# A SwiGLU's gate and up projections as a 2x2 block product with seven half products

## The chip, the cores and the metric

The kernel runs on one core of a Trainium2 chip. Its metric is the device time of one execution in microseconds. Five engines with queues of their own take part: TensorE (PE, matmuls, with its weight loads shown apart as PEld), VectorE (DVE), ScalarE (ACT), GpSimd (POOL) and SyncE (SP, which here only issues the transfers). The kernel has TensorE write into eight banks of PSUM, 128 x 512 float32 each; all other data is worked on in SBUF.

## The reference: what is computed

Two layers, each a feed-forward block (FFN1), a mixer and a second feed-forward block (FFN2), on 512 tokens of width 1024, all in float32. A feed-forward block is

```python
def swiglu_ffn(h, w_gate, w_up, w_down):
    return (jax.nn.silu(h @ w_gate) * (h @ w_up)) @ w_down
```

with h = rms_norm(x), w_gate and w_up of 1024 x 2816 and w_down of 2816 x 1024; its result is normalised again, halved and added to x. So each block has 22 column tiles of 128 (2816 = 22 x 128) in gate and in up. The mixer (attention, a convolution and gated linear attention, joined by gates) isn't touched by the change.

## The kernel before, in words

**Products in three parts.** The operands of most matmuls are of the type F32R, and float32 data is split in two for it: `split` (L109) casts it to F32R on ScalarE (`hi`, L110) and lets VectorE subtract that from the original (`lo`, L111). A product is hi x hi + hi x lo + lo x hi, three matmuls. The normalised input stands transposed in SBUF as `xh` and `xl` (L101, 102), 8 tiles of 128 of the width by 512 tokens.

**Weights.** `load_w` (L113) fetches 128 x 1024 float32 into `raw` (three buffers), and splits them into `whi` and `wlo` (five buffers each). `proj_cols` (L136) loads a column tile of 128, and `mm_cols` (L130) runs 8 x 3 matmuls of 128 x 128 stationary weights against 512 tokens, into one bank.

**A feed-forward block** is `ffn` (L267). Its first two column tiles go the other way round (L278 to 287): the tokens are stationary, 128 at a time, and 256 columns of weights move (`mm_tok`, L161, bank `pf`), since the input arrives token tile by token tile: `arrive[i]()` (L205) transposes token tile i on TensorE into banks `pt` and splits them into xh and xl, between the matmuls. The results `ht` are transposed later (L299). The other 20 column tiles are the loop of L289:

```python
pg = proj_cols(wg, f * P, "pg")
pu = proj_cols(wu, f * P, "pu")
nc.scalar.activation(h, pg, AF.Silu)
nc.vector.tensor_tensor(h, pu, h, op=ALU.mult)
```

The 22 results `hid` are then split by `stat` (L304) into `sh` and `sl` and multiplied with w_down in `out_proj` (L226), which keeps eight banks open, for four token tiles by two halves of the width. As each token tile ends there, `finish` (L831) applies the norm after the block, adds to x and starts the norm before the next block (`pre_norm`, L193).

**Buffers.** Tiles of 128 x 512 come from four groups of slots (L27): t 16, b 4, q 10, s 14. Banks come from two groups (L28): pa 2, pb 6. A slot or buffer is handed on when its last reader is done.

**Order.** Matmuls and transposes are held in the order of the text (L65 to 69). All other instructions are put in order at build time by the framework's planner, which goes by the order of the text among those whose inputs and buffers are free by its own estimate of times. Each engine then works its queue strictly in that order, and waits on semaphores where something is not ready. Transfers are all issued from SP's queue, in order as well.

Of the kernel before, what the change touches and what calls it, by code (L numbers as in the profile page):

```python
# [8 lines left out]
F32 = mybir.dt.float32  # L9
F32R = mybir.dt.float32r  # L10
AF = mybir.ActivationFunctionType
ALU = mybir.AluOpType

P = 128
D = 1024
S = 512
NT = S // P
KC = D // P
DFF = 2816
NF = DFF // P  # L20
# [21 lines left out]
def kernel(  # L42
# [9 lines left out]
    nc = tc.nc  # L52
# [5 lines left out]
    wp = ctx.enter_context(tc.tile_pool(name="wp", bufs=5))  # L58
    tp = ctx.enter_context(tc.tile_pool(name="tp", bufs=1))
# [5 lines left out]
    def mm(*a, **k):  # L65
        tc.keep_in_program_order(nc.tensor.matmul(*a, **k))  # L66

    def transpose(*a):
        tc.keep_in_program_order(nc.tensor.transpose(*a))

    def slot(name, dt=F32, tag="t"):
        return tp.tile([P, 512], dt, tag=tag, name=name, bufs=SLOTS[tag])

    def bank(n, tag="pb"):
        return psp.tile([P, 512], F32, tag=tag, name=n, bufs=BANKS[tag])


    ident = const.tile([P, P], F32, name="ident")
# [11 lines left out]
    for c in range(2):  # L90
        blk = strict[:, c * CHUNK:(c + 1) * CHUNK]
        r = slice(c * CHUNK, (c + 1) * CHUNK)
# [8 lines left out]
    xh = resid.tile([P, KC, S], F32R, name="xh")  # L101
    xl = resid.tile([P, KC, S], F32R, name="xl")
# [6 lines left out]
    def split(hi, lo, src):  # L109
        nc.scalar.copy(hi, src)  # L110
        nc.vector.tensor_tensor(lo, src, hi.bitcast(F32), op=ALU.subtract)  # L111

    def load_w(parts, n):  # L113
        raw = wp.tile([P, 1024], F32, tag="raw", name="raw", bufs=3)
        for view, src in parts:
            nc.sync.dma_start(view(raw), src)
        hi = wp.tile([P, 1024], F32R, tag="whi", name="whi")
        lo = wp.tile([P, 1024], F32R, tag="wlo", name="wlo")
        split(hi[:, :n], lo[:, :n], raw[:, :n])
        return hi, lo  # L120

    def load_cols(w2d, c0, width=P):
        kc = w2d.shape[0] // P
        n = kc * width
        hi, lo = load_w([(lambda r: r[:, :n].rearrange("p (k c) -> p k c", c=width),
                          w2d[:, c0:c0 + width].rearrange("(k p) c -> p k c", p=P))], n)
        v = lambda t: t[:, :n].rearrange("p (k c) -> p k c", c=width)
        return v(hi), v(lo)

    def mm_cols(ps, wh, wl, ks=range(KC)):  # L130
        for k in ks:
            mm(ps, wh[:, k, :], xh[:, k, :], start=(k == 0), stop=False)
            mm(ps, wh[:, k, :], xl[:, k, :], start=False, stop=False)
            mm(ps, wl[:, k, :], xh[:, k, :], start=False, stop=(k == KC - 1))

    def proj_cols(w2d, c0, name, tag="pb"):  # L136
        wh, wl = load_cols(w2d, c0)
        ps = bank(name, tag)
        mm_cols(ps, wh, wl)
        return ps  # L140
# [30 lines left out]
    def load_g(row):  # L171
        g = gp.tile([P, D], F32, tag="g", name="g")
        nc.sync.dma_start(g, row.unsqueeze(0).broadcast_to([P, D]))
        return g
# [5 lines left out]
    def rms(srcs):  # L180

        ss = sm.tile([P, 2], F32, tag="ss", name="ss")
        for h in range(2):
            nc.scalar.activation(junk, srcs[h], AF.Square, scale=1.0 / 32.0, accum_out=ss[:, h:h + 1])
        ms = sm.tile([P, 1], F32, tag="ms", name="ms")
        nc.vector.tensor_scalar(ms, ss[:, 0:1], ss[:, 1:2], EPS, op0=ALU.add, op1=ALU.add)
        rs = sm.tile([P, 1], F32, tag="rs", name="rs")
        nc.gpsimd.tensor_tensor(rs, ms, mhalf[:, 0:1], op=ALU.pow)
        return rs

    HS = [slice(h * HALF, (h + 1) * HALF) for h in range(2)]

    def pre_norm(i, gB, pooled=()):  # L193
        t = slice(i * P, (i + 1) * P)
        hns = [slot("hn", tag="b") for j in range(2)]
        for j in pooled:
            nc.gpsimd.tensor_tensor(hns[j], x_sb[i][:, HS[j]], gB[:, HS[j]], op=ALU.mult)
        rs = rms([x_sb[i][:, c] for c in HS])
        for j in range(2):
            if j in pooled:  # L200
                nc.scalar.mul(hns[j], hns[j], rs)
            else:
                nc.vector.scalar_tensor_tensor(hns[j], x_sb[i][:, HS[j]], rs, gB[:, HS[j]], op0=ALU.mult, op1=ALU.mult)

        def arrive():  # L205
            for j, hn in enumerate(hns):
                pt = bank("pt")
                for k in range(4):
                    transpose(pt[:, k * P:(k + 1) * P], hn[:, k * P:(k + 1) * P], ident)
                src = pt.rearrange("p (k t) -> p k t", t=P)  # L210
                split(xh[:, 4 * j:4 * j + 4, t], xl[:, 4 * j:4 * j + 4, t], src)

        return arrive

# [43 lines left out]
        return w  # L258


    def ffn_weights(wg, wu):
        return load_kcols(wg, 0, 256), load_kcols(wu, 0, 256)

    def mixer_weights(W):
        return load_kcols(W, C_V, 512)

    def ffn(wg, wu, wd, weights, arrive, finish, upcoming, early, begin):  # L267

        if begin is None:
            wgt, wut = weights  # L270
        else:
            wgt = load_kcols(wg, 0, 256)
            begin(0)
            wut = load_kcols(wu, 0, 256)
            begin(1)
            arrive[0]()
        hk = []
        for i in range(NT):  # L278
            pf = bank("pf", "pb")
            mm_tok(pf[:, 0:256], i, wgt)  # L280
            if i + 1 < NT:
                arrive[i + 1]()
            mm_tok(pf[:, 256:512], i, wut, first=False)
            h = slot("ht", tag="s")
            nc.scalar.activation(h[:, 0:256], pf[:, 0:256], AF.Silu)
            nc.vector.tensor_tensor(h[:, 0:256], pf[:, 256:512], h[:, 0:256], op=ALU.mult)
            hk.append(h)
        hid = [None, None]
        for f in range(2, NF):  # L289
            pg = proj_cols(wg, f * P, "pg")  # L290
            pu = proj_cols(wu, f * P, "pu")
            h = slot("hid", tag="t" if f < 18 else "q")
            nc.scalar.activation(h, pg, AF.Silu)
            nc.vector.tensor_tensor(h, pu, h, op=ALU.mult)  # L294
            hid.append(h)
            if f < 4:
                pt = bank("pth", "pa")
                for i in range(NT):
                    transpose(pt[:, i * P:(i + 1) * P], hk[i][:, (f - 2) * P:(f - 1) * P], ident)  # L299
                h = slot("hid", tag="q")  # L300
                nc.scalar.copy(h, pt)
                hid[f - 2] = h

        def stat(f):  # L304
            sh, sl = slot("sh", F32R, "s"), slot("sl", F32R, "s")
            split(sh, sl, hid[f])
            return sh, sl

        return out_proj(wd, NF, stat, TAIL, finish, upcoming, early)
# [500 lines left out]

    load_x(0)
    g0 = load_g(norm_pre[0, 0])
    arrive = [pre_norm(0, g0)]

    def begin(n):
        if n == 0:
            load_x(1)
            arrive.append(pre_norm(1, g0))
        else:
            load_x(2)  # L820
            load_x(3)
            arrive.extend(pre_norm(i, g0) for i in (2, 3))

    weights = None
    subs = [(l, s) for l in range(L) for s in range(3)]
    for idx, (l, s) in enumerate(subs):
        gpost = load_g(norm_post[l, s])
        gnext = load_g(norm_pre[subs[idx + 1][0], subs[idx + 1][1]]) if idx + 1 < len(subs) else None
        upcoming = []

        def finish(i, banks):  # L831
            post_norm(i, banks, gpost, 1.0 if s == 1 else 0.5)
            if gnext is not None:
                upcoming.append(pre_norm(i, gnext, (1,) if i < 2 else ()))
            else:
                for h in range(2):
                    nc.sync.dma_start(out[0, i * P:(i + 1) * P, HS[h]], x_sb[i][:, HS[h]])

        early = None
        if idx + 1 < len(subs):  # L840
            l1, s1 = subs[idx + 1]
            early = ((lambda: ffn_weights(f1g[l1], f1u[l1])), (lambda: mixer_weights(w_in[l1])),
                     (lambda: ffn_weights(f2g[l1], f2u[l1])))[s1]
        if s == 0:
            weights = ffn(f1g[l], f1u[l], f1d[l], weights, arrive, finish, upcoming, early,
                          begin if idx == 0 else None)
        elif s == 1:
            weights = mixer(l, weights, arrive, finish, upcoming, early)
        else:
            weights = ffn(f2g[l], f2u[l], f2d[l], weights, arrive, finish, upcoming, early, None)  # L850
        arrive = upcoming


# [27 lines left out]
```

## Time and profile before

| | |
|---|---|
| median of three timed runs | 2432.33 us (2432.09 to 2432.5) |
| the profiled execution, its own time | 2432.07 us |
| its span in the profile | 2430.0 us |
| TensorE busy / weight loads busy | 2410.4 us / 2013.2 us |
| VectorE busy | 1186.6 us |
| ScalarE busy | 846.1 us |
| mean granted TensorE clock | 0.998 |
| read from memory | 227.32 MB |

An engine's busy time counts its own instructions; the lengths of matmuls are modelled and overlap, so what one matmul costs is read from a stretch of many, length by count. The chain of waits goes back from the last instruction to what released each step, and shows so which engine set the end. "Idle before" in a row is the time that the engine stood still ahead of these instructions, with what ended it.

### The profile page before, as it was taken

How to read it: one execution, taken by the hardware profiler on the slowest of the kernel's cores; microseconds unless marked ns; L12 is line 12 of the kernel's file. 1: busy time of each engine (PE TensorE's matmuls, PEld its weight loads, DVE VectorE, ACT ScalarE, POOL GpSimd, SP SyncE). 2: the span in 40 equal slices, each digit the busy share in tenths (PEclk: the TensorE clock that was granted, in tenths of full speed). 3: DMA queues.
4: the chain of work that ended last, by engine and by line, in shares of the span. 5: the costliest groups of instructions: out<-in, count | busy, mean ns of one | idle time of the engine just before them, and what ended most of it. 6: DMA issues, size and time to landing. Idle time of an engine off the chain costs nothing.

```text
span 2430.0 us, 28558 instructions
## 1 busy us (share of the span) xinstructions
PE 2410.4 (99%) x11528; PEld 2013.2 (83%) x11528; DVE 1186.6 (49%) x1551; ACT 846.1 (35%) x1340; POOL 174.7 (7%) x282
## 2 busy tenths in 40 slices
PE   8999999999999999999999999999999999999998
PEld 7888888887888898888888888888878888888887
DVE  4322336858965353223353223378599644432233
ACT  4222226644323342222342222366433334322222
POOL 0000001201011100000000000012010211000000
PEclk9999999999999999999999999999999999999999
DMA  6333333231333243333243333241313332333331
GB/s 185 97 101 96 96 96 107 64 87 52 106 87 104 78 122 96 96 98 98 82 122 96 96 97 97 85 119 53 96 53 104 96 104 80 112 95 96 100 98 62
DMA packets 304692, 231.27 MB, mean 95 GB/s; under 512 B 9290, under 2 KB 281708, under 8 KB 304560
## 3 DMA queue, kind: packets, MB, share of 16 engines
q1 hardware_dynamic: 304560, 229.45, 32.1%
q8 instruction: 90, 1.47, 0.3%
q14 instruction: 42, 0.34, 0.0%
HBM read 227.32 MB, written 2.10 MB: 94 GB/s over the span
## 4 chain that ended last, share of the span: by engine, by line
PE 99%; ACT 0%; DMA 0%; DVE 0%; SPq 0%; issue 0%; DVEq 0%; POOLq 0%; ACTq 0%
PE o L66 23%; PE pu L66 18%; PE pg L66 18%; PE gate L66 11%; PE pb L66 5%; PE pf L66 4%; PE pa L66 2%; PE gr L66 2%; PE pv L66 2%; PE q L66 2%; PE gv L66 2%; PE k L66 2%; PE pgl L66 2%; PE gk L66 1%; PE gq L66 1%; PE z L66 1%
## 5 line engine op out<-in xcount | busy, mean ns | idle before, releaser
L110 ACT CAST whi<-raw 128x1024 fp32r<-128x1024 f32 x418 | 438.0, 1049 | 1033.5 <-PE pg L66 325.6
L111 DVE TENSOR_TENSOR wlo<-raw,whi 128x1024 fp32r<-128x1024 f32 x418 | 519.8, 1246 | 564.1 <-ACT whi L110 553.2
L66 PE MATMUL o<-whi,sh 128*128 128x512 f32 x704 | 274.1, 389 | 0.0
L66 PE MATMUL o<-whi,sl 128*128 128x512 f32 x704 | 273.9, 389 | 0.0
L66 PE MATMUL o<-wlo,sh 128*128 128x512 f32 x704 | 273.9, 389 | 0.0
L66 PE MATMUL pg<-xh,whi 128*128 128x512 f32 x640 | 249.8, 390 | 0.0
L66 PE MATMUL pg<-xh,wlo 128*128 128x512 f32 x640 | 249.1, 389 | 0.0
L66 PE MATMUL pg<-xl,whi 128*128 128x512 f32 x640 | 249.0, 389 | 0.0
L66 PE MATMUL pu<-xh,wlo 128*128 128x512 f32 x640 | 249.0, 389 | 0.0
L66 PE MATMUL pu<-xh,whi 128*128 128x512 f32 x640 | 249.0, 389 | 0.0
L66 PE MATMUL pu<-xl,whi 128*128 128x512 f32 x640 | 249.0, 389 | 0.0
L294 DVE TENSOR_TENSOR hid<-pu,hid 128x512 f32<-128x512 f32 x80 | 55.3, 692 | 273.5 <-PE pu L66 273.5
L481 DVE SCALAR_TENSOR_TENSOR y<-u,cw,y 128x511 f32<-128x511 f32 (+14 forms) x240 | 164.3, 747 | 0.0
L111 DVE TENSOR_TENSOR sl<-hid,sh 128x512 fp32r<-128x512 f32 x88 | 60.1, 690 | 198.0 <-ACT sh L110 198.0
L66 PEld LDWEIGHTS o<-whi,sl 128*128 128x128 f32 x704 | 132.1, 188 | 27.5
L66 PEld LDWEIGHTS o<-wlo,sh 128*128 128x128 f32 x704 | 132.1, 188 | 27.4
L66 PEld LDWEIGHTS o<-whi,sh 128*128 128x128 f32 x704 | 132.1, 188 | 27.3
L66 PE MATMUL gate<-xh,whi 128*128 128x512 f32 x384 | 151.3, 394 | 0.0
L66 PE MATMUL gate<-xl,whi 128*128 128x512 f32 x384 | 149.6, 390 | 0.0
L66 PE MATMUL gate<-xh,wlo 128*128 128x512 f32 x384 | 149.5, 389 | 0.0
L66 PEld LDWEIGHTS pu<-xh,wlo 128*128 128x128 f32 x640 | 120.1, 188 | 25.1
L66 PEld LDWEIGHTS pg<-xh,wlo 128*128 128x128 f32 x640 | 120.1, 188 | 25.0
(219 smaller groups left out, 3927.2 us busy)
## 6 DMA issues: line engine op xcount, KB each, us to landing
raw<-in_w_in_dram SPq DMA_DIRECT2D x108, 512.0 KB, 3.9
raw<-in_ffn_w_gate_dram SPq DMA_DIRECT2D x88, 512.0 KB, 3.9
raw<-in_ffn_w_up_dram SPq DMA_DIRECT2D x88, 512.0 KB, 3.9
raw<-in_ffn_w_down_dram SPq DMA_DIRECT2D x88, 512.0 KB, 3.5
raw<-in_w_branch_dram SPq DMA_DIRECT2D x24, 512.0 KB, 3.3
raw<-in_w_out_dram SPq DMA_DIRECT2D x16, 512.0 KB, 3.3
g<-in_norm_pre_dram SPq DMA_DIRECT2D x6, 512.0 KB
g<-in_norm_post_dram SPq DMA_DIRECT2D x6, 512.0 KB, 5.3
```

Of the source, the lines that this page charges most:

```text
L66: tc.keep_in_program_order(nc.tensor.matmul(*a, **k))
L110: nc.scalar.copy(hi, src)
L111: nc.vector.tensor_tensor(lo, src, hi.bitcast(F32), op=ALU.subtract)
L294: nc.vector.tensor_tensor(h, pu, h, op=ALU.mult)
L481: nc.vector.scalar_tensor_tensor(y[:, back:], u[:, :S - back], cw[:, c, j:j + 1], y[:, back:], op0=ALU.mult, op1=ALU.add)
```

## The change

Column tiles 3 to 21 (19 of 22) of gate and up are computed together, as one block product per tile. Let A11 and A12 be the upper and lower 512 rows of the gate's 128 columns, A21 and A22 those of up's, and B11, B21 the two halves of the width for tokens 0 to 255, B12, B22 for tokens 256 to 511. Wanted are gate = (A11 B11 + A12 B21, A11 B12 + A12 B22) and up likewise with A21 and A22: eight half products. The change forms

- S1 = A21 + A22, S2 = S1 + A11, S3 = A11 + A21, S4 = S2 + A12, from the weights, for each unit (a unit is one column tile);
- T1 = B11 - B12, T2 = -T1 - B22, T3 = T2 + B11, T4 = T2 + B21, from the input, once per block;
- seven products: A11 B11, S3 T3, S2 T2, A12 B21, S1 T1, A22 T4, S4 B22, each of 4 x 3 matmuls of 256 tokens.

Three banks A, B and C serve a unit. S2 T2, S1 T1 and S4 B22 are added in A to what A11 B11 has left there, and ScalarE copies A out after the first three of these four (p1, u2, u4), and C after S3 T3 (p7); A22 T4 is added in C. Three VectorE sums put the four results together, silu is applied to the two halves of gate, and one product ends the unit.

`Forms` holds the T: for the first two token tiles the transposes are kept in float32 (`xr`, ScalarE), for the last two VectorE makes the T tile by tile (16 sums of 128 x 256), and `finish` splits them (eight of 128 x 512), placed behind the transposes of the first two column tiles. T1 to T3 stand in 12 slots of the group s and T4 in the four of b until the last unit; the float32 forms and `xr` take 12 of the group t for a while.

`Ring` splits the seven sums and weights of a unit, two to a buffer of whi and wlo, so that a unit takes three and a half of these; the pairing of an even unit differs from that of an odd one. Raw weights come in two buffers of 3072 (one per unit, four transfers of 256 KB; elsewhere they are used in thirds) in place of three of 1024. The `unit`'s copies lie in two new tiles `cp`. Column tile 2 stays as it was, and the transposes of the first two tiles stand between its gate and its up. The buffer for descriptors that the framework sets aside in SBUF is made smaller.

```diff
--- before.py
+++ after.py
@@ -110,10 +110,20 @@
         nc.scalar.copy(hi, src)
         nc.vector.tensor_tensor(lo, src, hi.bitcast(F32), op=ALU.subtract)
 
-    def load_w(parts, n):
-        raw = wp.tile([P, 1024], F32, tag="raw", name="raw", bufs=3)
+    thirds = []
+
+    def load_raw(parts):
+        if not thirds:
+            r = wp.tile([P, 3, 1024], F32, tag="raw", name="raw", bufs=2)
+            thirds.extend(r[:, j] for j in range(3))
+        raw = thirds.pop(0)
         for view, src in parts:
             nc.sync.dma_start(view(raw), src)
+        return raw
+
+    def load_w(parts, n):
+        raw = load_raw(parts)
         hi = wp.tile([P, 1024], F32R, tag="whi", name="whi")
         lo = wp.tile([P, 1024], F32R, tag="wlo", name="wlo")
         split(hi[:, :n], lo[:, :n], raw[:, :n])
...
         def arrive():
+            pts = []
             for j, hn in enumerate(hns):
                 pt = bank("pt")
                 for k in range(4):
                     transpose(pt[:, k * P:(k + 1) * P], hn[:, k * P:(k + 1) * P], ident)
                 src = pt.rearrange("p (k t) -> p k t", t=P)
                 split(xh[:, 4 * j:4 * j + 4, t], xl[:, 4 * j:4 * j + 4, t], src)
+                pts.append(src)
+            if forms is not None:
+                forms.arrive(i, pts)
 
         return arrive
...
+    class Forms:
+        def __init__(self):
+            self.first = []
+            self.raw = None
+            self.parts = {}
+
+        def arrive(self, i, pts):
+            if i < 2:
+                row = [slot("xr").rearrange("p (k t) -> p k t", t=P) for src in pts]
+                for r, src in zip(row, pts):
+                    nc.scalar.copy(r, src)
+                self.first.append(row)
+                return
+            if self.raw is None:
+                self.raw = {n: [slot(n).rearrange("p (k t) -> p k t", k=2) for c in range(2)]
+                            for n in ("T1", "T2", "T3", "T4")}
+            first = self.first[i - 2]
+            tok = slice((i - 2) * P, (i - 1) * P)
+            for c in range(2):
+                k = slice(2 * c, 2 * c + 2)
+                t1, t2 = (self.raw[n][c][:, :, tok] for n in ("T1", "T2"))
+                nc.vector.tensor_tensor(t1, first[0][:, k], pts[0][:, k], op=ALU.subtract)
+                nc.vector.scalar_tensor_tensor(t2, t1, -1.0, pts[1][:, k], op0=ALU.mult, op1=ALU.subtract)
+                for j, n in enumerate(("T3", "T4")):
+                    nc.vector.tensor_tensor(self.raw[n][c][:, :, tok], t2, first[j][:, k], op=ALU.add)
+
+        def finish(self):
+            for n, tag in (("T3", "s"), ("T2", "s"), ("T1", "s"), ("T4", "b")):
+                hi = [slot(n + "h", F32R, tag).rearrange("p (k t) -> p k t", k=2) for c in range(2)]
+                lo = [slot(n + "l", F32R, tag).rearrange("p (k t) -> p k t", k=2) for c in range(2)]
+                for c in range(2):
+                    split(hi[c], lo[c], self.raw[n][c])
+                self.parts[n] = [(hi[k // 2][:, k % 2], lo[k // 2][:, k % 2]) for k in range(4)]
+            for n, k0, t0 in (("B11", 0, 0), ("B21", 4, 0), ("B22", 4, 256)):
+                self.parts[n] = [(xh[:, k0 + k, t0:t0 + 256], xl[:, k0 + k, t0:t0 + 256]) for k in range(4)]
+
+    class Ring:
+        def __init__(self):
+            self.n = 0
+
+        def put(self, src):
+            two = len(src.shape) == 3
+            if self.n % 2 == 0:
+                self.hi, self.lo = (wp.tile([P, 1024], F32R, tag=t, name=t).rearrange("p (f c) -> p f c", f=2)
+                                    for t in ("whi", "wlo"))
+            h = self.n % 2
+            assert not (two and h)
+            self.n += 2 if two else 1
+            f = slice(0, 2) if two else slice(h, h + 1)
+            split(self.hi[:, f], self.lo[:, f], src if two else src.unsqueeze(1))
+            v = lambda t: t.rearrange("p (k c) -> p k c", c=P)
+            r = [(v(self.hi[:, j]), v(self.lo[:, j])) for j in range(f.start, f.stop)]
+            return r if two else r[0]
+
+    H0, H1 = slice(0, 256), slice(256, 512)
+
+    def unit(w0, w1, c0, forms, ring, h):
+        r = wp.tile([P, 6, 512], F32, tag="raw", name="raw", bufs=2)
+        for w, q0 in ((w0, 0), (w1, 2)):
+            for j in range(2):
+                nc.sync.dma_start(r[:, q0 + 3 * j].rearrange("p (k c) -> p k c", c=P),
+                                  w[j * 512:(j + 1) * 512, c0:c0 + P].rearrange("(k p) c -> p k c", p=P))
+        add = lambda o, a, b: nc.vector.tensor_tensor(o, a, b, op=ALU.add)
+        add(r[:, 1:5:3], r[:, 0:6:5], r[:, 2:3].broadcast_to([P, 2, 512]))
+        add(r[:, 2], r[:, 4], r[:, 0])
+        A, B, C = bank("A"), bank("B"), bank("C")
+
+        def product(w, n, ps, first):
+            wh, wl = w
+            for k, (fh, fl) in enumerate(forms.parts[n]):
+                for j, (a, b) in enumerate(((wh, fh), (wh, fl), (wl, fh))):
+                    mm(ps[:, H0], a[:, k], b, start=(first and k == 0 and j == 0), stop=False, skip_group_check=True)
+
+        cp = [tp.tile([P, 512], F32, tag="cp", name="cp", bufs=2) for _ in range(2)]
+        p1, p7, u2, u4 = cp[0][:, H0], cp[0][:, H1], cp[1][:, H0], cp[1][:, H1]
+        put = ring.put
+        even = ring.n % 2 == 0
+        if even:
+            a11, s3 = put(r[:, 0:2])
+            s2, a12 = put(r[:, 2:4])
+        else:
+            a11 = put(r[:, 0])
+            s3, s2 = put(r[:, 1:3])
+        product(a11, "B11", A, True)
+        nc.scalar.copy(p1, A[:, H0])
+        add(r[:, 0], r[:, 2], r[:, 3])
+        if even:
+            s1, a22 = put(r[:, 4:6])
+        else:
+            a12, s1 = put(r[:, 3:5])
+        product(s3, "T3", C, True)
+        nc.scalar.copy(p7, C[:, H0])
+        product(s2, "T2", A, False)
+        nc.scalar.copy(u2, A[:, H0])
+        if even:
+            s4 = put(r[:, 0])
+        else:
+            s4, a22 = put(r[:, 0:6:5])
+        product(a12, "B21", B, True)
+        add(h[:, H0], B[:, H0], p1)
+        nc.scalar.activation(h[:, H0], h[:, H0], AF.Silu)
+        product(s1, "T1", A, False)
+        nc.scalar.copy(u4, A[:, H0])
+        product(a22, "T4", C, False)
+        nc.vector.tensor_tensor(u2, C[:, H0], u2, op=ALU.subtract)
+        nc.vector.tensor_tensor(u4, p7, u4, op=ALU.subtract)
+        product(s4, "B22", A, False)
+        nc.scalar.activation(h[:, H1], A[:, H0], AF.Silu)
+        nc.vector.tensor_tensor(h, cp[1], h, op=ALU.mult)
...
-        hid = [None, None]
-        for f in range(2, NF):
-            pg = proj_cols(wg, f * P, "pg")
-            pu = proj_cols(wu, f * P, "pu")
-            h = slot("hid", tag="t" if f < 18 else "q")
-            nc.scalar.activation(h, pg, AF.Silu)
-            nc.vector.tensor_tensor(h, pu, h, op=ALU.mult)
-            hid.append(h)
-            if f < 4:
-                pt = bank("pth", "pa")
-                for i in range(NT):
-                    transpose(pt[:, i * P:(i + 1) * P], hk[i][:, (f - 2) * P:(f - 1) * P], ident)
-                h = slot("hid", tag="q")
-                nc.scalar.copy(h, pt)
-                hid[f - 2] = h
+        hid = [None] * NF
+        ring = Ring()
+
+        def turn(f):
+            pt = bank("pth", "pa")
+            for i in range(NT):
+                transpose(pt[:, i * P:(i + 1) * P], hk[i][:, f * P:(f + 1) * P], ident)
+            hid[f] = slot("hid", tag="q")
+            nc.scalar.copy(hid[f], pt)
+
+        pg = proj_cols(wg, 2 * P, "pg")
+        turn(0)
+        turn(1)
+        forms.finish()
+        pu = proj_cols(wu, 2 * P, "pu")
+        hid[2] = slot("hid")
+        nc.scalar.activation(hid[2], pg, AF.Silu)
+        nc.vector.tensor_tensor(hid[2], pu, hid[2], op=ALU.mult)
+        thirds.clear()
+        for f in range(3, NF):
+            hid[f] = slot("hid", tag="t" if f < 18 else "q")
+            unit(wg, wu, f * P, forms, ring, hid[f])
...
+        here, forms = forms, Forms() if s != 0 else None
+        ahead = forms
+
+        def finish(i, banks, ahead=ahead):
             post_norm(i, banks, gpost, 1.0 if s == 1 else 0.5)
             if gnext is not None:
-                upcoming.append(pre_norm(i, gnext, (1,) if i < 2 else ()))
+                upcoming.append(pre_norm(i, gnext, (1,) if i < 2 else (), ahead))
...
-    nc = _bacc.Bacc("TRN2", target_bir_lowering=False, num_devices=1)
+    nc = _bacc.Bacc("TRN2", target_bir_lowering=False, num_devices=1, dynamic_dma_scratch_size=1024)
```

More of the change, by code (lines that the diff above doesn't have):

```diff
@@ L191, with pre_norm @@
     HS = [slice(h * HALF, (h + 1) * HALF) for h in range(2)]
-    def pre_norm(i, gB, pooled=()):
+    def pre_norm(i, gB, pooled=(), forms=None):
         t = slice(i * P, (i + 1) * P)
@@ L265, in mixer_weights, with ffn @@
         return load_kcols(W, C_V, 512)
-    def ffn(wg, wu, wd, weights, arrive, finish, upcoming, early, begin):
+    def ffn(wg, wu, wd, weights, forms, arrive, finish, upcoming, early, begin):
         if begin is None:
@@ L812 @@
     g0 = load_g(norm_pre[0, 0])
-    arrive = [pre_norm(0, g0)]
+    forms = form0 = Forms()
+    arrive = [pre_norm(0, g0, forms=forms)]
     def begin(n):
@@ L817, in begin @@
             load_x(1)
-            arrive.append(pre_norm(1, g0))
+            arrive.append(pre_norm(1, g0, forms=form0))
         else:
@@ L821, in begin @@
             load_x(3)
-            arrive.extend(pre_norm(i, g0) for i in (2, 3))
+            arrive.extend(pre_norm(i, g0, forms=form0) for i in (2, 3))
     weights = None
@@ L829 @@
         upcoming = []
-        def finish(i, banks):
+        here, forms = forms, Forms() if s != 0 else None
+        ahead = forms
+        def finish(i, banks, ahead=ahead):
             post_norm(i, banks, gpost, 1.0 if s == 1 else 0.5)
             if gnext is not None:
-                upcoming.append(pre_norm(i, gnext, (1,) if i < 2 else ()))
+                upcoming.append(pre_norm(i, gnext, (1,) if i < 2 else (), ahead))
             else:
@@ L844 @@
         if s == 0:
-            weights = ffn(f1g[l], f1u[l], f1d[l], weights, arrive, finish, upcoming, early,
+            weights = ffn(f1g[l], f1u[l], f1d[l], weights, here, arrive, finish, upcoming, early,
                           begin if idx == 0 else None)
@@ L849 @@
         else:
-            weights = ffn(f2g[l], f2u[l], f2d[l], weights, arrive, finish, upcoming, early, None)
+            weights = ffn(f2g[l], f2u[l], f2d[l], weights, here, arrive, finish, upcoming, early, None)
         arrive = upcoming
```

## The prediction

> **What bounds the kernel now.** I read the page's first part, the slices and the chain of waits first, to see which engine sets the end; then the chain in windows, to price one matmul; last the groups of instructions and the timeline, to price the other engines.
>
> ```profile
> span 2430.0 us, 28558 instructions
> PE 2410.4 (99%) x11528; PEld 2013.2 (83%) x11528; DVE 1186.6 (49%) x1551; ACT 846.1 (35%) x1340; POOL 174.7 (7%) x282
> ...
> PE 99%; ACT 0%; DMA 0%; DVE 0%; SPq 0%; issue 0%; DVEq 0%; POOLq 0%; ACTq 0%
> PE o L66 23%; PE pu L66 18%; PE pg L66 18%; PE gate L66 11%; PE pb L66 5%; PE pf L66 4%; PE pa L66 2%; PE gr L66 2%; PE pv L66 2%; PE q L66 2%; PE gv L66 2%; PE k L66 2%; PE pgl L66 2%; PE gk L66 1%; PE gq L66 1%; PE z L66 1%
> ```
>
> TensorE is the chain from end to end, and pg and pu, the gate and up projections that the change rewrites, are 36% of it. The other engines are half idle. So a change pays if it shortens the row of matmuls, and costs what it makes that row wait.
>
> The chain inside a feed-forward block shows the price of a column tile, and the chain at its start and in the mixer shows matmuls with narrower moving operands (pf 256 columns, gk 272). Columns: start, length, what, count.
>
> ```profile
> 106.34 5.44 PE pg L66 x24
> 111.78 5.44 PE pu L66 x24
> ...
> 477.76 9.07 PE gk L66 x72
> ...
> 1224.69 5.94 PE pf L66 x48
> 1230.64 0.87 PE pt L69 x8
> 1231.51 5.75 PE pf L66 x48
> 1237.26 0.87 PE pt L69 x8
> 1238.13 8.63 PE pf L66 x72
> ```
>
> With 512 columns a matmul takes 5.44/24 = 226.7 ns from start to start; with 256, 8.63/72 = 119.9 (5.75/48 = 119.8); with 272, 9.07/72 = 126.0. The 389 ns that a group prints for a 512-column matmul is its length with overlap, and isn't summed. From 256 to 512 columns is 106.9 ns more, 0.418 ns a column, so some 13 ns belong to the matmul and not to its columns. The scheme doubles the matmuls per product of the same size, and so pays those 13 ns twice.
>
> **The change, part by part.** *Matmuls.* A column tile was 2 x 8 x 3 = 48 matmuls of 512 columns: 10.88 us (5.44 + 5.44). It becomes 7 products x 4 x 3 = 84 of 256 columns: 84 x 119.8 = 10.06 us. Gain 0.82 us. Tiles 3 to 21 are 19, in four feed-forward blocks: 76 units, **-62.1 us**. The first three column tiles and their eight transposes stay.
>
> Here a rule of the Trainium skill, "TensorE: Matmul & The Clock Gate", section "Back-to-back issue gap", says N/2.4 + 2.5 ns per warm matmul: 215.8 and 109.2 ns. By it a unit would go from 10.36 to 9.17 us, and the sum would be -90 us; the rows have 10.9 and 10.6 ns more than the rule in each matmul, so it isn't used for the sum.
>
> *VectorE.* The prices:
>
> ```profile
> L111 DVE TENSOR_TENSOR wlo<-raw,whi 128x1024 fp32r<-128x1024 f32 x418 | 519.8, 1246 | 564.1 <-ACT whi L110 553.2
> ...
> L294 DVE TENSOR_TENSOR hid<-pu,hid 128x512 f32<-128x512 f32 x80 | 55.3, 692 | 273.5 <-PE pu L66 273.5
> ```
>
> ```profile
> L286 DVE TENSOR_TENSOR ht<-pf,ht 128x256 f32<-128x256 f32 x16 | 6.7, 421 | 14.1 <-ACT ht L285 14.1
> ```
>
> ```profile
> 1222.08 2.36 DVE L111 TENSOR_TENSOR wlo<-raw,whi 128x1024 fp32r<-128x1024 f32 x2
> ...
> 1271.07 1.89 DVE L111 TENSOR_TENSOR sl<-hid,sh 128x512 fp32r<-128x512 f32 x3
> ```
>
> A tile had two splits and a product, 2 x 1.246 + 0.692 = 3.2 us. A unit has one 1024-wide weight sum, two 512-wide ones, splits of 7 x 512 (three of 1024, one of 512), three 256-wide sums of results and the 512-wide product: 4 x 1.246 + 4 x 0.69 + 3 x 0.42 = 9.0 us. By durations that is 89% of 10.06. Two in a row overlap (two of 1024 in 2.36 us, so 2.36 - 1.22 = 1.14 each; three of 512 in 1.89, so 0.60 each), and with 0.33 for 256 columns the load is 4 x 1.14 + 4 x 0.60 + 3 x 0.33 = 8.0 us, 79%. It is hidden as long as each split is done before its product. A pair of halves shares one of five buffers, so a split can be made some eight products (8 x 12 x 0.12 = 11.5 us) ahead. That TensorE lives with a VectorE as full as this shows in the mixer:
>
> ```profile
> core 0: us, PE busy (x) PEld busy (x) DVE busy (x) ACT busy (x) POOL busy (x), PEclk, DMA share, GB/s
> ...
> 620.00:680.00 60.00, 60.00 (x294) 48.55 (x293) 57.87 (x90) 20.82 (x46) 2.91 (x4) 1.00 0.38 106
> ```
>
> Taken at 0 (below: 0; above: rival 1).
>
> *ScalarE, and the one new wait on the path.* Four copies of a bank are added, and TensorE waits for three of them: it adds the next product to bank A after p1, u2 and u4 are copied, with one product in another bank between (12 x 0.12 = 1.44 us). Matmuls keep the order of the text, so everything behind on TensorE waits too.
>
> ```profile
> 1234.41 0.38 ACT L285 ACTIVATE ht<-pf 128x256 f32<-128x256 f32 x1 [2.23 <-PE pf L66]
> ...
> 1263.41 1.05 ACT L110 CAST whi<-raw 128x1024 fp32r<-128x1024 f32 x1 [3.75 <-PE pg L66]
> 1264.36 0.59 ACT L293 ACTIVATE hid<-pg 128x512 f32<-128x512 f32 x1
> ```
>
> The first row is a 256-wide read of a bank: up of that token tile ends at 1231.51 + 24 x 0.12 = 1234.38, the read starts 0.03 later and takes 0.38, so an idle ScalarE leaves 1.44 - 0.41 = 1.0 us. The other rows are the danger: a cast of later weights, released by the last matmuls of the tile, went first, and the evacuation followed 0.95 us behind. Then the copy ends 0.95 + 0.38 = 1.33 us after the cast's start, just inside 1.44. Load: 3.5 casts x 1.05, four copies and two activations x 0.38: 6.0 of 10.06 us. One cast ahead costs nothing, two cost 2 x 0.95 + 0.38 - 1.44 = 0.84 us. Bounds per unit: 0 and 3 x 0.84; I take 0.1 us, near the low end, since a tile's buffer is freed once per two products and two casts rarely stand together: 76 x 0.1 = **+7.6 us**.
>
> *Entry of a block.* ScalarE copies four more 512-wide transposes (x read for the first two token tiles), VectorE makes 16 sums of 256 for the last two, then eight 512-wide splits on both.
>
> ```profile
> 1215.00:1225.00 10.00, 10.00 (x67) 9.07 (x66) 9.80 (x16) 8.99 (x19) 1.40 (x3) 1.00 0.21 61
> 1225.00:1235.00 10.00, 10.00 (x85) 9.86 (x84) 7.74 (x14) 3.57 (x9) 1.71 (x2) 1.00 0.83 254
> 1235.00:1245.00 10.00, 10.00 (x86) 10.00 (x86) 3.20 (x6) 3.55 (x5) 0.00 (x0) 1.00 0.02 5
> 1245.00:1255.00 10.00, 10.00 (x52) 8.55 (x51) 5.23 (x5) 4.03 (x5) 0.00 (x0) 1.00 0.74 210
> ```
>
> Sums and splits, 16 x 0.42 + 8 x 0.69 = 12.2 us of VectorE, fall from 1231 to 1260, where it is a third to half busy: 0. The first copies fall into 1215 to 1225, where VectorE has 9.80 and ScalarE 8.99 of 10 us and the last token tile's norm, which both carry, is already on time by little (the 5.94 of the first pf piece against 5.75 is a 0.19 us stall). Two copies of 0.58 ahead of that norm make it 1.16 us late: 3 entries x 1.16 = **+3.5 us**; the first block waits for its input and counts 0. Bounds: 0, and all 12.2 us exposed.
>
> *Leaving a block, transfers, the rest.* T1 to T3 hold 12 of 14 "s" slots to the last unit, so one stationary pair is ready for the down projection and the second is made while the first works (24 x 226.7 ns = 5.4 us against 0.62 + 0.69): 0, bounds 0 and 1.3 us x 4. Bytes stay; a unit's MB has a unit's time, 10 us, and a 512 KB transfer lands in 3.9:
>
> ```profile
> raw<-in_ffn_w_gate_dram SPq DMA_DIRECT2D x88, 512.0 KB, 3.9
> ```
>
> Two more issues a unit on SP wait behind nothing but weights. Raw buffers go from three to two of three thirds, never fewer ahead than before: 0, and at best the idle of TensorE, 2430.0 - 2410.4 = 19.6 us in all.
>
> Sum against the profiled execution, 2432.07 us (2430.0 and 2.07 around it; the median is 0.26 above): 2432.07 - 62.1 + 7.6 + 3.5 = 2381.1. **Forecast 2381 us**, 2.1% less.
>
> **The rivals.** (1) *VectorE becomes the bound; slower.* In a chain weight sum, cast, split, each of the eleven operations can start only after another engine's result, 0.21 us late as here, and pays its full length:
>
> ```profile
> 1244.99 1.22 DVE L111 TENSOR_TENSOR wlo<-raw,whi 128x1024 fp32r<-128x1024 f32 x1 [0.21 <-ACT whi L110]
> ```
>
> Then a unit is 9.0 + 11 x 0.21 = 11.3 us, 76 x 0.4 = 30 more than now: 2432 + 30 + 3.5 = 2466. It decides from 10.06 us of VectorE time a unit, and makes the kernel slower from 10.83. For it: VectorE's queue is in order, an evacuation at its head blocks the splits, and the order is fixed before the run. Against: overlap, and eight products of lead. (2) *ScalarE's copies come late.* With two casts ahead of one copy in every second unit: 38 x 0.84 = 32 us, 2432 - 62 + 32 + 3.5 = 2405. (3) *The entries are exposed*: 4 x 12.2 = 49 us, 2419. Against: the third and fourth window. (4) *Seven products aren't cheaper than eight.* In the units the weights are stationary and x moves, the reverse of pf; at 10.88/84 = 129.5 ns a matmul the gain is nil, 2432. For: only 9.7 ns of distance. Against: gk's 126.0 with 272 columns, and pg, stationary weights, fits the same line. (5) *Weight loads bound.* 84 loads in place of 48, and
>
> ```profile
> L66 PEld LDWEIGHTS pf<-wlo,xh 128*128 128x128 f32 x256 | 49.6, 194 | 0.8 <-DVE wlo L111 0.7
> ```
>
> end to end they would take 84 x 0.194 = 16.3 us a unit: 76 x 5.4 = 410 more, 2842. Against: 48 pf loads passed in 5.75 us. The Trainium skill, "Perfetto Trace Analysis", section "Identifying the Most-Contended Engine", judges TensorE's headroom by this busy share, and by it 83% would leave no room for more loads; the window with 86 loads, 10.00 of 10.00 busy, at 119.8 ns a matmul differs. (6) *The 13 ns of a matmul vanish in the units*: 84 x 256 x 0.418 = 8.99 us, 76 x 1.89 = 144 less, 2432 - 144 + 11 = 2299. Against: pf and gk, stretches as dense, both pay them. The first page named above speaks for a part of it, and by its rule the time would be 2432 - 90 + 11 = 2353.
>
> **How the numbers follow.** Forecast 0.64, its own range 2366 (no stalls, 4 us gained elsewhere) to 2396 (0.3 us a unit); rivals: (1) 0.13, (2) 0.12, (3) 0.05, (4) 0.04, (5) 0.01, (6) 0.01. The range goes from 2364 to 2428, to hold (2) and (3), and leaves out (1), (4), (5) and (6): 0.19. Faster by more than 0.2% (about what a measurement of this kernel can tell from no change): 0.64 + 0.12 + 0.05 + 0.01 = 0.82; within 0.2%: 0.04; slower: 0.14.
>
> **What would show it.** Products of 12 matmuls at 1.44 us in the chain, units of 10.1 to 10.2 us; VectorE at 8 to 9 tenths in the units with no wait of TensorE on its splits. Rival 1 shows as waits of TensorE on wlo, rival 2 as waits on the copies of bank A, rival 3 as holes in pf and before the first unit, rivals 4 and 5 as a pitch over 126 ns with no wait. It is wrong if units take over 10.4 us, or if the four starts of the units lose more than 3 us each.

## The result and the profile after

The changed kernel takes 2450.96 us (median of four runs, 2448.87 to 2453.86) against 2432.21 before: a ratio of 1.0081 (95% interval 1.0063 to 1.0098). It is slower by 0.8%, where 2.1% less was forecast, and lies outside the range.

First the page's opening lines of the kernel after:

```profile
span 2449.7 us, 35818 instructions
PE 2376.6 (97%) x14264; PEld 2103.7 (86%) x14264; DVE 1614.6 (66%) x2255; ACT 1093.4 (45%) x1920; POOL 174.1 (7%) x282
```

TensorE was busy for 99% of the span and is now at 97%, so it waits. What for is in the groups of instructions (last columns: idle time ahead of the group, and what ended it):

```profile
L350 DVE TENSOR_TENSOR raw<-raw 128x512 f32<-128x512 f32 (+1 forms) x228 | 197.6, 867 | 170.8 <-DMA raw<-in_ffn_w_up_dram 168.5
...
L66 PE MATMUL A<-xh,whi 128*128 128x256 f32 x608 | 178.9, 294 | 53.1 <-ACT cp L390 53.1
```

TensorE waits 53 us for line 390, the copy u4; and VectorE waits 169 us for the last transfer of a unit's raw weights, in the weight sums of that unit (`raw<-raw`; the 1024-wide one makes S1 and S3 together). Neither row exists in the kernel before.

From the starts of the matmuls in the trace, the parts of the run are (us, four feed-forward blocks where four numbers stand):

| | before | after | after - before |
|---|---|---|---|
| stationary tokens, first pf to first pg | 28.30, 25.68, 25.81, 25.67 | 29.18, 25.91, 26.52, 25.91 | +2.1 |
| column tiles 2 to 21, first pg to first o | 218.58 in each | 223.39, 222.17, 223.85, 222.61 | +17.7 |
| mixers without their output projections | 432.47, 429.51 | 430.95, 431.07 | 0.0 |

Nearly all of the loss stands in the column tiles, which should have become 15.5 us shorter per block (19 x 0.82) and became 4.4 longer. So about 20 us a block, 1.05 a unit, went somewhere inside the units. Per product, from its first matmul to the first of the next, mean over the 76 units (the seventh and the next unit's first share bank A and can't be parted; 12 matmuls of 119.8 ns are 1.44):

| product (bank) | S3 T3 (C) | S2 T2 (A) | A12 B21 (B) | S1 T1 (A) | A22 T4 (C) | S4 B22, next A11 B11 (A) |
|---|---|---|---|---|---|---|
| after, us | 1.47 | 1.48 | 1.45 | 1.49 | **2.27** | 2.96 |
| queued matmuls alone | 1.44 | 1.44 | 1.44 | 1.44 | 1.44 | 2.88 |

The matmuls themselves cost what the rows of pf said. The hole is between A22 T4 and S4 B22: 0.83 us a unit, where a unit takes 11.2 us in the mean. 64 of the 76 units have it. The last two of each block never do, and the first only in one block of the four.

Here is one such hole, in order of time: first SP's queue, then VectorE, ScalarE and TensorE of the kernel after.

```profile
117.32 0.92 SPq L348 DMA_DIRECT2D raw<-in_ffn_w_gate_dram  x2
118.28 1.06 SPq L348 DMA_DIRECT2D raw<-in_ffn_w_up_dram  x2
```

```profile
120.00 0.69 DVE L396 TENSOR_TENSOR hid<-cp,hid 128x512 f32<-128x512 f32 x1
123.63 1.23 DVE L350 TENSOR_TENSOR raw<-raw 128x1024 f32<-128x1024 f32 x1 [2.95 <-DMA raw<-in_ffn_w_up_dram]
124.77 1.22 DVE L111 TENSOR_TENSOR wlo<-raw,whi 128x1024 fp32r<-128x1024 f32 x1
125.91 0.42 DVE L350 TENSOR_TENSOR hid<-B,cp 128x256 f32<-128x256 f32 x1
```

```profile
123.48 1.05 ACT L110 CAST whi<-raw 128x1024 fp32r<-128x1024 f32 x1 [0.95 <-PE B L66]
126.36 0.42 ACT L388 ACTIVATE hid<-hid 128x256 f32<-128x256 f32 x1 [1.83 <-DVE hid L350]
126.69 0.35 ACT L390 COPY cp<-A 128x256 f32<-128x256 f32 x1
```

```profile
124.84 0.28 PE L66 MATMUL C<-T4h,whi 128*128 128x256 f32 x1
...
126.16 0.28 PE L66 MATMUL C<-T4h,wlo 128*128 128x256 f32 x1
127.09 0.39 PE L66 MATMUL A<-xh,whi 128*128 128x256 f32 x1 [0.65 <-ACT cp L390]
127.31 0.28 PE L66 MATMUL A<-xl,whi 128*128 128x256 f32 x1
```

VectorE stands still for 2.95 us with the weight sum of the unit *two ahead* at the head of its queue: the four transfers of that unit were issued from 117.32 to 119.34 and are there at 123.6. Behind the sum stand a split and the sum from bank B, whose product ended at 123.40; it starts at 125.91, 2.5 us late. (A product's end is taken here as the start of the next one.) On ScalarE silu waits for it, and behind silu stands u4, whose product was done at 124.84 and which runs at 126.69. TensorE, due to go on in bank A at 126.28, goes on at 127.09.

The other units agree. In each of the 64 the hole is the lateness of the sum from B less 1.70 to 1.80 us (here 2.51 - 0.81), and in the 12 without a hole that sum is at most 1.47 us late. The last two units of a block have no unit two ahead whose weight sum could stand in front: there it is 0.85 and 0.63 us late.

### The profile page after: what moved, and what is told of

Same layout as the page of the kernel before. It is cut to its first block, busy times and chain, and to the rows that moved or that the text cites. A ratio compares the mean times of both kernels' runs of the same rounds, so it can differ in the third digit from the quotient of the medians.

```text
span 2449.7 us, 35818 instructions
## 1 busy us (share of the span) xinstructions
PE 2376.6 (97%) x14264; PEld 2103.7 (86%) x14264; DVE 1614.6 (66%) x2255; ACT 1093.4 (45%) x1920; POOL 174.1 (7%) x282
## 5 line engine op out<-in xcount | busy, mean ns | idle before, releaser
L111 DVE TENSOR_TENSOR wlo<-raw,whi 128x1024 fp32r<-128x1024 f32 (+2 forms) x570 | 663.5, 1167 | 262.3 <-ACT whi L110 256.3
L110 ACT CAST whi<-raw 128x1024 fp32r<-128x1024 f32 (+2 forms) x570 | 561.3, 991 | 577.4 <-PE gate L66 122.5
L350 DVE TENSOR_TENSOR raw<-raw 128x512 f32<-128x512 f32 (+1 forms) x228 | 197.6, 867 | 170.8 <-DMA raw<-in_ffn_w_up_dram 168.5
L66 PE MATMUL A<-xh,whi 128*128 128x256 f32 x608 | 178.9, 294 | 53.1 <-ACT cp L390 53.1
L66 PEld LDWEIGHTS A<-xh,whi 128*128 128x128 f32 x608 | 116.2, 191 | 66.1 <-ACT cp L390 66.0
L66 PE MATMUL A<-xh,wlo 128*128 128x256 f32 x608 | 172.2, 283 | 0.0
L66 PE MATMUL A<-xl,whi 128*128 128x256 f32 x608 | 172.1, 283 | 0.0
L110 ACT CAST sh<-hid 128x512 fp32r<-128x512 f32 x88 | 54.5, 624 | 233.3 <-PE o L66 232.4
L66 PEld LDWEIGHTS A<-xl,whi 128*128 128x128 f32 x608 | 116.6, 192 | 0.2
L66 PEld LDWEIGHTS A<-xh,wlo 128*128 128x128 f32 x608 | 116.5, 192 | 0.0
```

Of the source, the lines that this page charges most:

```text
L350: add = lambda o, a, b: nc.vector.tensor_tensor(o, a, b, op=ALU.add)
```

## The experiments

Three theories went in. A is the chain just told: a transfer holds up VectorE, VectorE holds up silu, silu holds up u4, and u4 holds up TensorE. B is that VectorE is full, the first rival of the prediction. C is casts ahead of the copies on ScalarE, its second. Unless said otherwise, the base is the changed kernel, and the ratio is to the kernel before. Diffs are cut at `...`.

**Only ScalarE's order** (`e1_act`):

```diff
-        nc.scalar.activation(h[:, H0], h[:, H0], AF.Silu)
         product(s1, "T1", A, False)
-        nc.scalar.copy(u4, A[:, H0])
+        c4 = nc.scalar.copy(u4, A[:, H0])
+        with tc.issue_after(c4.ins):
+            nc.scalar.activation(h[:, H0], h[:, H0], AF.Silu)
```

> One edit on ScalarE's queue: silu of the gate's first half stands behind the copy u4 and not ahead of it; all sums, splits and transfers as in the changed kernel. Theory A (u4 is late because silu stands ahead of it and waits for VectorE's sum from bank B, which stands behind a weight sum that waits for its transfer): the sixth product's 2.27 us in the changed kernel falls to 1.44 to 1.55, so 76 x 0.75 = 57 us come back, 2451 - 57 = 2394 (2380 to 2405). Theory B (VectorE is full, 9.0 us and more a unit): the lateness only moves to a later wait, 2440 to 2455. Theory C (casts of weights ahead of the copies on ScalarE): no cast is moved, 2440 to 2455.

Measured 2400.28 us (ratio 0.9874, 0.9857 to 0.9890), 51 us less than the changed kernel. The product A22 T4 is at 1.44 us as A said. But S3 T3 rose from 1.47 to 1.67 in the mean, with 3.15 at most. VectorE and ScalarE of this kernel at that longest one, where S2 T2, due at 146.30, starts at 148.01:

```profile
141.78 1.23 DVE L350 TENSOR_TENSOR raw<-raw 128x1024 f32<-128x1024 f32 x1 [3.88 <-DMA raw<-in_ffn_w_up_dram]
142.93 1.22 DVE L111 TENSOR_TENSOR wlo<-raw,whi 128x1024 fp32r<-128x1024 f32 x1
144.06 0.68 DVE L350 TENSOR_TENSOR raw<-raw 128x512 f32<-128x512 f32 x1
144.66 0.42 DVE L350 TENSOR_TENSOR hid<-B,cp 128x256 f32<-128x256 f32 x1
```

```profile
145.11 0.42 ACT L391 ACTIVATE hid<-hid 128x256 f32<-128x256 f32 x1 [4.00 <-DVE hid L350]
145.44 1.03 ACT L110 CAST whi<-raw 128x1024 fp32r<-128x1024 f32 x1
146.38 0.37 ACT L396 ACTIVATE hid<-A 128x256 f32<-128x256 f32 x1
146.65 1.03 ACT L110 CAST whi<-raw 128x1024 fp32r<-128x1024 f32 x1
147.58 0.37 ACT L372 COPY cp<-A 128x256 f32<-128x256 f32 x1
```

The transfer still holds up VectorE, and silu still waits for the sum from B, 4 us here. Now it is no longer u4 that stands behind silu but two casts, the second silu and p1 of the next unit, and TensorE waits for p1. So silu's place carried the delay in the changed kernel and isn't its source.

**Only VectorE's order** (`e2_dve`), the weight sum of unit n+2 behind the sum from bank B of unit n; `behind` adds an edge of issue order, with no wait, and `evac` lists the block's sums from B so far:

```diff
...
-        add(r[:, 1:5:3], r[:, 0:6:5], r[:, 2:3].broadcast_to([P, 2, 512]))
+        ones = add(r[:, 1:5:3], r[:, 0:6:5], r[:, 2:3].broadcast_to([P, 2, 512]))
+        if len(evac) > 1:
+            behind(ones, evac[-2])
...
-        add(h[:, H0], B[:, H0], p1)
+        evac.append(add(h[:, H0], B[:, H0], p1))
...
```

> One edit on VectorE's queue: the first weight sum of unit n+2 stands behind unit n's sum from bank B and not ahead of it; ScalarE's text as in the changed kernel. Theory A: the sum from B starts within 0.2 us of the end of its product, silu is done before S1 T1 ends, the seventh product waits no more: 2385 to 2405. Theory B: 2440 to 2455, since no work is taken from VectorE. Theory C: 2440 to 2455. If only the order on ScalarE counts, this stays at 2451 while the other edit gains.

Measured 2380.63 us (0.9786, 0.9771 to 0.9801): 70 us less than the changed kernel by an edge on one instruction a unit, and 2.1% less than before. This kernel is called the mended one below. VectorE and ScalarE at the same unit as above:

```profile
118.85 0.42 DVE L356 TENSOR_TENSOR hid<-B,cp 128x256 f32<-128x256 f32 x1 [0.69 <-PE B L66]
119.19 1.22 DVE L356 TENSOR_TENSOR raw<-raw 128x1024 f32<-128x1024 f32 x1
```

```profile
119.68 0.41 ACT L396 ACTIVATE hid<-hid 128x256 f32<-128x256 f32 x1
120.29 0.37 ACT L398 COPY cp<-A 128x256 f32<-128x256 f32 x1 [0.19 <-PE A L66]
```

Now VectorE waits for the product and not for the transfer, and here u4 waits for its own product alone. The weight sum follows with no wait: the transfer had landed by then. In the whole run VectorE's weight sums wait 4 us for transfers, and not 169. The sum from B starts 0.20 us after its product in every second unit, as expected, and up to 0.85 us after it in the others, behind a split. A block's column tiles take 205.59 us in all four blocks, a unit 10.19 or 10.23. The planner also moved what needs the weight sum's result, and in every second unit it put one 512-wide cast ahead of u4. B falls, since no work was taken from VectorE, and C, since no cast left its place ahead of a copy and one more came there.

**Both orders** (`e3_both`), the two edits together:

> Both edits. Theory A: each alone takes away the same wait, so both together are within 8 us of the better one, 2380 to 2400, and a unit takes 10.1 to 10.3 us. Theory B: 2440 to 2455.

Measured 2381.25 us (0.9790, 0.9775 to 0.9805), the same as the edit on VectorE alone, and the lengths of all products are equal too. Once VectorE is on time, silu's place costs nothing.

**A shorter transfer** (`e5_three`). A22 is not loaded, and A12 takes its place in S1 and in A22 T4:

```diff
-            for j in range(2):
+            for j in range(2 if q0 == 0 else 1):
                 nc.sync.dma_start(r[:, q0 + 3 * j].rearrange("p (k c) -> p k c", c=P),
...
-        add(r[:, 1:5:3], r[:, 0:6:5], r[:, 2:3].broadcast_to([P, 2, 512]))
+        add(r[:, 1:5:3], r[:, 0:6:3], r[:, 2:3].broadcast_to([P, 2, 512]))
...
```

> Three transfers a unit in place of four: A22 is not loaded and A12 stands in its place (the result is then another). The queues' order is left to the planner. Theory A: the last transfer of a unit is issued 0.5 us earlier and moves a quarter less, so the weight sum and all behind it start 1.0 us earlier, and the sixth product falls from 2.27 to 1.5: 76 x 0.75 = 57 us less, 2385 to 2405. Theories B and C: engines have the same work, 2440 to 2455.

Measured 2398.28 us (one run), 53 us less than the changed kernel, with the weight sums still ahead of the sums from B in the queue. A22 T4 falls from 2.27 to 1.66. SP and VectorE at the same unit as above:

```profile
113.84 0.92 SPq L348 DMA_DIRECT2D raw<-in_ffn_w_gate_dram  x2
114.80 0.51 SPq L348 DMA_DIRECT2D raw<-in_ffn_w_up_dram  x1
```

```profile
119.05 1.22 DVE L350 TENSOR_TENSOR raw<-raw 128x1024 f32<-128x1024 f32 x1 [1.06 <-DMA raw<-in_ffn_w_up_dram]
120.19 1.22 DVE L111 TENSOR_TENSOR wlo<-raw,whi 128x1024 fp32r<-128x1024 f32 x1
121.32 0.68 DVE L350 TENSOR_TENSOR raw<-raw 128x512 f32<-128x512 f32 x1
121.92 0.42 DVE L350 TENSOR_TENSOR hid<-B,cp 128x256 f32<-128x256 f32 x1
```

The weight sum starts 5.2 us after the unit's first issue (119.05 - 113.84) and not 6.3 (123.63 - 117.32). The planner put one instruction more between it and the sum from B, a weight sum or a split, and the sum from B is still only 1.2 us late here. So with the same work on all engines the time fell with the transfer, although the order grew worse.

**A longer transfer** (`e6_five`), one of 256 KB more ahead of the four:

```diff
+        nc.sync.dma_start(r[:, 1].rearrange("p (k c) -> p k c", c=P),
+                          w0[0:512, c0:c0 + P].rearrange("(k p) c -> p k c", p=P))
         for w, q0 in ((w0, 0), (w1, 2)):
```

> The changed kernel with a fifth transfer of 256 KB per unit ahead of the four, into a place that the weight sum overwrites. Theory A (a weight sum that waits for its transfer delays the sum from bank B behind it): the last transfer is issued 0.5 us later and has 0.25 MB more in front, so the wait before the seventh product grows by 0.5 to 1.5 us a unit: 2451 + 76 x 1.0 = 2525 (2490 to 2560). Without theory A, transfers being elsewhere off the path: 2445 to 2460.

Measured 2441.51 us (one run): not some 75 us more but 9 less, so the numbers expected with theory A and without it were both missed. The transfer is later as meant, and the weight sum starts 7.3 us after the unit's first issue (126.28 - 119.00) in place of 6.3 (123.63 - 117.32):

```profile
119.00 0.37 SPq L346 DMA_DIRECT2D raw<-in_ffn_w_gate_dram  x1
```

```profile
124.10 1.23 DVE L111 TENSOR_TENSOR wlo<-raw,whi 128x1024 fp32r<-128x1024 f32 x1 [1.01 <-ACT whi L110]
126.28 1.23 DVE L352 TENSOR_TENSOR raw<-raw 128x1024 f32<-128x1024 f32 x1 [0.95 <-DMA raw<-in_ffn_w_up_dram]
127.42 0.42 DVE L352 TENSOR_TENSOR hid<-B,cp 128x256 f32<-128x256 f32 x1
```

But the planner made another order with it: the split that stood between the weight sum and the sum from B now stands ahead of both in every second unit, as here, where it uses VectorE's idle time, and behind both in the others. In the unit shown the sum from B is 1.6 us late (its product ended at 125.82) and A22 T4 keeps its 1.44 us; the unit after it has a hole of 1.45 (2.89 - 1.44). So what counts is the whole lateness of the sum from B, wait and the work stacked up behind the wait together, and here too up to some 1.7 us of it are free. How the 9 us divide between the new order and the later landing wasn't parted.

**The longer transfer in the mended order** (`e8_e2_five`), the same fifth transfer, with the edit on VectorE's queue:

> The fifth transfer in the kernel with the edit on VectorE's queue. Theory A: behind the sum from bank B the weight sum has time, so the same delay of the transfers costs little, 2379 to 2395, where the kernel without the edit loses 40 us or more. If the transfers themselves were the bound (weights late for their products): as much as there.

Measured 2383.54 us (one run), 3 us more than without it, with units of 10.18 to 10.24. The column tiles of a block take 205.54 to 205.56 us, no more than without it, so the 3 us stand outside the units. The fifth transfer costs the units nothing where it holds up nobody.

**How full VectorE may be** (`e9_e2_load`), with the edit on VectorE's queue, S4's sum four times over:

```diff
-        add(r[:, 0], r[:, 2], r[:, 3])
+        add(r[:, 0], r[:, 2], r[:, 3])
+        add(r[:, 0], r[:, 2], r[:, 3])
+        add(r[:, 0], r[:, 2], r[:, 3])
+        add(r[:, 0], r[:, 2], r[:, 3])
```

(S4 is then A12 + S2 as before, since the sum doesn't read its own place.)

> The kernel with the edit on VectorE's queue, with S4's sum made four times in a unit in place of once: 3 x 0.60 = 1.8 us more of VectorE by their spacing, 3 x 0.69 = 2.1 by their length. By spacing a unit has 8.0 + 1.8 = 9.8 us of VectorE in 10.2 of TensorE: hidden, 2379 to 2400. By length it has 9.0 + 2.1 = 11.1: 76 x 0.9 = 68 us more, 2435 to 2460.

Measured 2382.52 us (one run), 2 us more than the mended kernel, as expected by spacing. The busy time of the engines over the same 100 us of the first block, for the changed kernel, for the edit on VectorE's queue, and for this run (PE, PEld, DVE, ACT, POOL, each with its count, then clock, DMA share, GB/s):

```profile
110.00:210.00 100.00, 91.65 (x738) 89.15 (x737) 72.20 (x98) 48.93 (x88) 0.00 (x0) 1.00 0.31 88
```

```profile
110.00:210.00 100.00, 100.00 (x826) 99.28 (x825) 80.44 (x108) 55.80 (x99) 0.00 (x0) 1.00 0.37 106
```

```profile
110.00:210.00 100.00, 100.00 (x826) 99.26 (x825) 98.32 (x139) 54.87 (x99) 0.00 (x0) 1.00 0.37 106
```

At 98% VectorE still holds up nothing in this stretch, with 826 matmuls in the 100 us as at 80%. In the whole run one unit of the 76 has a hole, of 0.57 us. In the changed kernel it is at 72% and TensorE at 92%: the slow kernel has the idler VectorE.

**The casts behind the copies as well** (`e7_casts`). The edit on VectorE's queue, and for even units three casts queued behind the copies p1, u2 and u4 of the unit before. For odd units the cast of A11 is queued behind the u4 of two units before as well. `copies` lists the copies p1, u2 and u4 of the units so far:

```diff
...
-        put = ring.put
+        def put(x, after=None, back=1):
+            if after is None or len(copies) < back:
+                return ring.put(x)
+            with tc.issue_after(copies[-back][after].ins):
+                return ring.put(x)
...
-            s2, a12 = put(r[:, 2:4])
+            s2, a12 = put(r[:, 2:4], 0)
...
-            a11 = put(r[:, 0])
+            a11 = put(r[:, 0], 2, 2)
...
-            s1, a22 = put(r[:, 4:6])
+            s1, a22 = put(r[:, 4:6], 1)
...
-            s4 = put(r[:, 0])
+            s4 = put(r[:, 0], 2)
...
```

> The edit on VectorE's queue, and on ScalarE the casts for even units stand behind the copies p1, u2 and u4 of the unit before, ahead of which they went. If the 0.13 us a unit over 84 x 0.1198 come from a copy that waits behind one cast (0.95 us), the products of 1.50 and 1.54 us become 1.44 and a unit 10.08: 2380.6 - 76 x 0.13 = 2371 (2368 to 2376). If they come from something else: 2378 to 2383.

Measured 2373.42 us (2368.55 to 2375.31; 0.9754, 0.9740 to 0.9767), the fastest of all kernels here, 2.5% less than before. Its chain:

```profile
114.48 1.44 PE C L66 x12
115.92 1.44 PE A L66 x12
117.36 1.44 PE B L66 x12
118.80 1.44 PE A L66 x12
120.24 1.44 PE C L66 x12
121.68 2.88 PE A L66 x24
```

Every product of every unit is at 1.44 and a unit at 10.08, so what the mended kernel still had over that were copies behind one cast. A block's column tiles take 203.31 us, 2.28 less than in the mended kernel or 0.12 a unit; 218.58 - 19 x 0.82 was 203.0. In every second unit the planner also put silu behind u4; by `e3_both` silu's place costs nothing in this order.

## Why the prediction was wrong

*The matmuls, -62.1 us: right.* 84 x 119.8 ns is 10.06 us, and the best kernel's units take 10.08. With weights stationary and tokens moving the pitch is that of pf, so rival 4 falls, and so does rival 6, since the 13 ns of each matmul are all there. The page "TensorE: Matmul & The Clock Gate" of the Trainium skill, section "Back-to-back issue gap", gives N/2.4 + 2.5 ns for the gap of an isolated warm matmul and says that a stream with weight loads goes by other figures. By that formula a unit would be 9.17 us; the best kernel's 10.08 differ.

*VectorE, taken at 0: here is the step that failed.* "It is hidden as long as each split is done before its product" looked only at the splits, the work that VectorE does ahead of TensorE, and at their sum. It left out that the sum from bank B stands in the same queue, that silu waits for it, and that silu stood ahead of u4, for which the prediction itself had 1.0 us to spare. The transfer term failed with it: "a unit's MB has a unit's time, 10 us, and a 512 KB transfer lands in 3.9" is throughput, and it named no instruction that stands behind the one that waits for the transfer. The one that waits, the weight sum, stood up to 4 us at the head of VectorE's queue, and behind it stood the sum from B. Cost: 70 us, which an edge on the weight sum alone gives back (2450.96 - 2380.63).

*Rival 1 had the size and not the cause.* It put a unit at 11.3 us, and units took 11.2. But it had an evacuation at the queue's head that blocks the splits, on a VectorE without room. It was the reverse: a sum that no product needed yet blocked the evacuation (in the mended kernel it is done at 120.4, and the products of its unit begin at 133.3), on a VectorE at 72%, and at 98% next to nothing is lost. The load itself was right: 79% by spacing was worked out, 80.4% measured; the lengths in the rows, summed, gave 89%, and the run with S4's sum four times over goes by the spacing.

*ScalarE, +7.6 us: too small in the changed kernel, and near by luck in the mended one.* This was the term for TensorE's waits on the copies of bank A, and it looked at casts alone. In the changed kernel the hole where TensorE waits for u4 makes 76 x 0.83 = 63 us, through silu and not through casts. In the mended kernel a unit has 0.15 us over 10.06, 11 us in all, where 0.1 was taken, but for another reason: "One cast ahead costs nothing" was wrong. One cast in front of a copy costs up to 0.1 us each time, and no two casts in a row held up a copy there. In the mended kernel rival 2's mechanism exists at that price only.

*Entry, +3.5 us: the measured change is +2.1,* but put together otherwise. The piece of pf that was to lose 1.16 us lost 0.23 to 0.25 in each of the three later blocks; the first block, counted at 0, lost 0.9, and the last piece of one block 0.5. Rival 3 falls. *Weight loads (rival 5):* they are 100% busy in the best kernel and TensorE still keeps its pitch:

```profile
110.00:210.00 100.00, 100.00 (x836) 100.00 (x835) 80.95 (x110) 56.40 (x100) 0.00 (x0) 1.00 0.37 106
```

836 matmuls in 100 us are 119.6 ns each. By the Trainium skill's "Perfetto Trace Analysis", section "Identifying the Most-Contended Engine", this share, beside the use of the peak, shows the room that is left; here 83% left room for 75% more loads a unit.

The forecast of 2381 us is what the scheme gives with one more edge in a queue, 2380.63; as it was changed, it isn't. That the two agree to 1 us is luck in part: in the mended kernel the column tiles gain 52.0 us where 54.5 were forecast (62.1 - 7.6), and the entries lose 1.8 where 3.5 were.

## What to carry to other kernels

Sum an engine's load, and then also list, for each instruction that waits for a transfer, what stands behind it in its queue and who waits for that; here an engine at 72% held up the kernel and at 98% it did not. An order that a planner fixes ahead rests on its estimate of when transfers land. Work that can wait, but hangs on a transfer, is better put behind the evacuations of banks by an explicit edge, as here. Look in the queues for the first instruction with a wait, not for the fullest engine.

## What the runs showed of the hardware that was not expected

A matmul that had to wait costs more than its wait. In the hole above, the next one starts 0.22 us after it (127.31 - 127.09) and not 0.12. It is so behind all 64 holes of the changed kernel, and the two products there take 2.97 to 2.98 us in place of 2.88. In the mended kernel, where a copy ended just in time, products took 1.50 to 1.54 us with no idle time in the rows, and 1.44 with the copy well ahead. This was 0.12 us a unit, 9 us of the kernel (4 x 2.28), and it shows in no list of waits. Why the second matmul is late is not shown by any run here.
